# ConvFFN entry of a hybrid decoder layer: weight sums of three units and the t4 operand on GpSimd, the first unit's sums made beside the output projection

## Chip, cores and metric

The kernel runs on one core of one Trainium2 chip. The metric is the device time of one execution in microseconds, lower is better. A difference of 0.3% (5.0 us here) is about what a measurement of this kernel can tell from no change.

## What is computed

One layer of a decoder with 1024 positions of width 1024. Three token mixers run on the same normalised input, their outputs are gated and summed, one output projection adds to the residual stream, and a gated MLP with a causal convolution of width 3 (the ConvFFN) follows. The change lies where the output projection ends and the ConvFFN begins:

```
x = x + merged @ w_o[l]

h = _rmsnorm(x, g_ffn[l])
u = _causal_dwconv(h @ w_up[l], ff_conv_w[l], ff_conv_b[l])
u_val, u_gate = jnp.split(u, 2, axis=-1)
x = x + (jax.nn.silu(u_gate) * u_val) @ w_down[l]
```

All of it is float32. `w_up` is 1024 x 5632, so `h @ w_up` has 44 row blocks of 128 in the kernel's transposed layout.

## The kernel before

Activations lie transposed: 128 channels on the partitions, positions along the free dimension, in two halves of 512 positions (`hs(1)` upper, `hs(0)` lower). A float32 product is made of three matmuls (`mm3`, L142 to L144) of operands split into a rounded high part (L129, ScalarE, "ACT") and the rest (L130, VectorE, "DVE"). One matmul handles 128 x 128 weights and 512 positions.

**Output projection** (L1079 to L1111). For `h` = 1, then 0, eight row blocks `d` of `w_o` go through `proj`; `ev(d)` adds the residual (L1088), stores it and collects the sum of squares (L1094, L1095). When a half is done, `rstd_rows` makes the row scale: `rstd` sums with eight small matmuls (L158), DVE scales (L148), GpSimd ("POOL") takes the power -1/2 (L150), and `spread` writes four diagonal pieces (L170, DVE) and multiplies them with ones (L172, PE), so that the scale of each position lies on all partitions, in PSUM. For the upper half the normalised pages `full` are made beside the lower half's products (`h2_upper`, L1072); for the lower half they can be made only after its last product.

**ConvFFN** (L1118 to L1177). `ffn_up(f)` for f = 0 to 21 is a unit: it makes two row blocks (value and gate) for both halves with seven half-size products instead of eight (Strassen-Winograd, `seven`, L672 to L720). Products `au` and `bu` need only the upper half's activations. The others need four operands made of both halves, each two pages of 128 x 1024 that are then split: `t3` is the lower minus the upper half (`diff`), `t2` is `full + diff` (L1149), `t1` is L1160, `t4` is L1166; `bl` is the lower half itself (L1158). On the weight side a unit needs three sums of its 128 x 512 weight quarters and one more later, all on DVE:

```
s1 = half()
nc.vector.tensor_add(s1, a2, b2)       # L695
nc.vector.tensor_sub(a2, a1, a2)       # L696
nc.vector.tensor_sub(a1, s1, a1)       # L697
...
nc.vector.tensor_sub(b1, b1, a1)       # L708
```

(L695 is `s1`, operand of `t1`; L696 that of `t3`; L697 that of `t2`; L708 that of `bl`.) The splits of weights go through a ring of two `whi` and two `wlo` buffers (`qring`).

The first three units are written interleaved (L1142 to L1170): the upper products of all three, then t2 and t3 of units 0 and 1, then t1, then bl and t4, then the rest of unit 2. From unit 3 on the loop at L1172 runs one unit after another. The order on each engine is set by a scheduler; `tc.high_priority` moves pieces forward. All transfers are issued by the SP queue in order.

Of the kernel before, what the change touches and what calls it, by code (L numbers as in the profile page):

```python
# [11 lines left out]
F32R = mybir.dt.float32r  # L12
# [30 lines left out]
def tile_hybrid_layer(ctx: ExitStack, tc: tile.TileContext, xT, memT, vecs, w_t, w_n, w_kv, w_if,  # L43
# [20 lines left out]
    BUFS = {"h": 16, "pg": 16, "U": 5, "y": 2, "raw": 2, "whi": 2, "wlo": 2, "hf": 4, "me": 2,  # L64
# [3 lines left out]
    def T(shape, tag, dt=F32, bufs=None):  # L68
        pool = {"mw": mlp, "mst": mlp, "px": late[0]}.get(tag, sb)
        return pool.tile(shape, dt, tag=tag, name=nm(tag), bufs=bufs or BUFS[tag])  # L70

# [577 lines left out]
    RAWS = [itertools.chain(("raw", "raw", "pg"), itertools.repeat("raw"))]  # L649
# [22 lines left out]
    def seven(w1, w2, x, done, urgent=False):  # L672

        tag = next(RAWS[0])
        if tag == "me":
            a1, b1 = T([P, HALF], tag), T([P, HALF], tag)
            nc.sync.dma_start(a1, w1[:, hs(0)])
            nc.sync.dma_start(b1, w1[:, hs(1)])
        else:
            r1 = T([P, S], tag)  # L680
            nc.sync.dma_start(r1, w1)
            a1, b1 = r1[:, hs(0)], r1[:, hs(1)]
        r2 = T([P, S], "pg")
        nc.sync.dma_start(r2, w2)
        a2, b2 = r2[:, hs(0)], r2[:, hs(1)]
        L, p2 = bank(turn(2, LONG)), bank(turn(3, SHORT))
        prod(L, qring(a1), x["au"])
        c1 = wide()
        up, lo = c1[:, hs(1)], c1[:, hs(0)]
        nc.scalar.activation(up, L, AF.Copy)  # L690
        prod(p2, qring(b1), x["bu"])
        nc.vector.tensor_add(up, up, p2)
        with tc.high_priority(offset=1000 if urgent else 0):
            s1 = half()
            nc.vector.tensor_add(s1, a2, b2)  # L695
            nc.vector.tensor_sub(a2, a1, a2)  # L696
            nc.vector.tensor_sub(a1, s1, a1)  # L697
        yield
        prod(L, qring(a1, 1000 if urgent else SOON), x["t2"], False)
        c2 = wide()  # L700
        nc.scalar.activation(c2[:, hs(1)], L, AF.Copy)
        R = bank(turn(3, SHORT))
        prod(R, qring(a2, 1000 if urgent else SOON), x["t3"])
        yield
        prod(L, qring(s1), x["t1"], False)
        nc.scalar.activation(c2[:, hs(0)], L, AF.Copy)
        nc.vector.tensor_add(c2[:, hs(0)], c2[:, hs(0)], R)
        nc.vector.tensor_sub(b1, b1, a1)  # L708
        yield
        prod(L, qring(b1), x["bl"], False)  # L710
        nc.scalar.activation(lo, L, AF.Copy)
        done(0, c1)
        prod(R, qring(b2), x["t4"], False)
        nc.vector.tensor_add(c2[:, hs(1)], c2[:, hs(1)], R)  # L714
        done(1, c2)
        yield
# [360 lines left out]
    diff = [page("h") for _ in range(2)]  # L1077
    for h in (1, 0):
# [24 lines left out]
        for d in range(KT):  # L1103
            proj(w_o[d], m_hi, m_lo, ev(d), halves=(h,))
# [10 lines left out]
    RAWS[0] = itertools.chain(("raw", "raw", "me"), itertools.cycle(("px", "px", "raw", "raw", "me")))  # L1115
    LONG[:], SHORT[:] = ["pj", "tr"], ["pv", "z"]

    def ffn_up(f):  # L1118
# [15 lines left out]
        return seven(w_up[f], w_up[NF + f], fx, done, f == 0)  # L1134
# [3 lines left out]
    for n, tag in (("t2", "h"), ("t3", "pg"), ("t1", "h"), ("bl", "pg"), ("t4", "h")):  # L1138
        fd[n], fx[n] = doubles(tag)
# [273 lines left out]
```

## Time and profile before

| | |
|---|---|
| median of 3 runs | 1662.75 us (1659.86 to 1664.12) |
| profiled execution | 1658.55 us |
| its span, first to last instruction | 1656.8 us |
| granted TensorE clock, mean | 0.999 of 2.4 GHz |
| busy: PE, DVE, ACT, POOL | 1635.1, 1212.9, 823.5, 93.3 us |
| end of the last product of the output projection | 1014.25 us in the span |
| first product of unit 3 | 1074.46 us in the span |

The profiled execution is 4.2 us below the median of the runs. A PE row in the timeline starts when its matmul starts; matmuls are pipelined, so the distance of two starts is the cost of one and the busy time of one (0.39 us) is longer. On DVE too the next instruction starts some 0.07 us before the one ahead has ended, so the distance of starts is used.

### The profile page before, as it was taken

To read this page: it belongs to the slowest core of one execution; us is meant where nothing else is said; L and a number is where in the kernel's file an instruction comes from. 1 tells how busy PE (TensorE), PEld (TensorE's weight loads), DVE (VectorE), ACT (ScalarE), POOL (GpSimd) and SP (SyncE) were. 2 spreads that over 40 slices of the span, in tenths; PEclk is the share of its full clock that TensorE was granted. 3 is DMA by queue.
4 is the path that set the end of the run, shared out by engine and by line. 5 is a ranking of instruction groups with operands and counts; after the bars stand their busy time and mean duration, and the time that the engine had idled before them with its cause. 6 is when DMAs were issued, how large, how long until landed. Compare 5 with 4: busy or idle time off the path is not lost.

```text
span 1656.8 us, 21182 instructions
## 1 busy us (share of the span) xinstructions
PE 1635.1 (99%) x7911; PEld 1333.6 (80%) x7911; DVE 1212.9 (73%) x1709; ACT 823.5 (50%) x1249; POOL 93.3 (6%) x157
## 2 busy tenths in 40 slices
PE   8999999999999999999999999999999999999999
PEld 4777888887877888888788887788888888788887
DVE  5649888768764666766557558987788777889764
ACT  4547777545554454666312344555555555543431
POOL 1002222020000010100000000000000000000000
PEclk9999999999999999999999999999999999999999
DMA  8420111423333665424854453322222221586132
GB/s 297 152 65 21 39 39 53 139 84 140 130 109 124 204 182 186 135 96 135 283 189 155 137 180 122 113 103 83 71 77 79 100 77 51 181 314 241 42 125 81
DMA packets 96249, 212.68 MB, mean 128 GB/s; under 512 B 12416, under 2 KB 36224, under 8 KB 96148
## 3 DMA queue, kind: packets, MB, share of 16 engines
q1 hardware_dynamic: 96148, 211.35, 37.5%
q8 instruction: 62, 1.02, 0.2%
q14 instruction: 39, 0.32, 0.1%
HBM read 156.71 MB, written 54.61 MB: 128 GB/s over the span
## 4 chain that ended last, share of the span: by engine, by line
PE 87%; DVE 3%; ACT 1%; DMA 1%; issue 0%; POOLq 0%; POOL 0%; ACTq 0%
PE ps_pj L142 13%; PE ps_pj L143 13%; PE ps_pj L144 13%; PE ps_pv L143 6%; PE ps_pv L142 6%; PE ps_pv L144 6%; PE ps_tr L142 4%; PE ps_tr L144 4%; PE ps_tr L143 4%; PE ps_z L142 3%; PE ps_z L143 3%; PE ps_z L144 3%; PE ps_pv L443 2%; PE ps_tr L429 2%; PE ps_z L403 1%; PE ps_z L404 1%
## 5 line engine op out<-in xcount | busy, mean ns | idle before, releaser
L143 PE MATMUL ps_pj<-h,whi 128*128 128x512 f32 x620 | 242.4, 391 | 0.0
L129 ACT ACTIVATE whi<-raw 128x512 fp32r<-128x512 f32 (+1 forms) x112 | 93.7, 837 | 176.3 <-PE ps_pj L143 81.9
L142 PE MATMUL ps_pj<-h,whi 128*128 128x512 f32 x412 | 165.0, 400 | 0.0
L142 PE MATMUL ps_pj<-pg,whi 128*128 128x512 f32 x396 | 154.8, 391 | 0.3 <-DVE pg L1053 0.2
L144 PE MATMUL ps_pj<-pg,wlo 128*128 128x512 f32 x380 | 147.9, 389 | 0.0
L143 PEld LDWEIGHTS ps_pj<-h,whi 128*128 128x128 f32 x620 | 116.7, 188 | 23.0 <-DVE U L280 0.2
L144 PE MATMUL ps_pj<-h,wlo 128*128 128x512 f32 x332 | 130.3, 392 | 0.0
L812 DVE SCALAR_TENSOR_TENSOR y<-U,vec,y 128x1023 f32<-128x1023 f32 x88 | 112.3, 1278 | 8.4 <-ACT y L810 8.4
L417 DVE TENSOR_TENSOR_SCAN U<-U 128x512 f32<-128x512 f32 (+3 forms) x96 | 92.9, 1008 | 17.5 <-POOL U L412 15.8
L142 PEld LDWEIGHTS ps_pj<-h,whi 128*128 128x128 f32 x412 | 77.6, 188 | 15.5 <-issue 0.3
L130 DVE TENSOR_TENSOR wlo<-raw,whi 128x1024 fp32r<-128x1024 f32 x54 | 65.9, 1221 | 32.2 <-ACT whi L129 32.0
L142 PEld LDWEIGHTS ps_pj<-pg,whi 128*128 128x128 f32 x396 | 74.4, 188 | 16.6 <-DVE pg L1053 0.8
L144 PEld LDWEIGHTS ps_pj<-pg,wlo 128*128 128x128 f32 x380 | 71.4, 188 | 14.8 <-issue 0.2
L129 ACT ACTIVATE whi<-pg 128x512 fp32r<-128x512 f32 (+1 forms) x59 | 43.4, 738 | 72.3 <-issue 21.1
L143 PE MATMUL ps_pj<-pg,whi 128*128 128x512 f32 x188 | 73.4, 390 | 0.0
L144 PEld LDWEIGHTS ps_pj<-h,wlo 128*128 128x128 f32 x332 | 62.6, 189 | 13.2
L143 PE MATMUL ps_pv<-h,whi 128*128 128x512 f32 x164 | 64.0, 390 | 0.0
L810 ACT ACTIVATE y<-U,vec 128x1024 f32<-128x1024 f32 x44 | 54.6, 1241 | 15.8 <-DVE U L714 14.4
L144 PE MATMUL ps_pj<-h,whi 128*128 128x512 f32 x156 | 60.8, 390 | 0.0
L406 ACT ACTIVATE U<-ps_z 128x1024 f32<-128x1024 f32 (+3 forms) x48 | 39.0, 813 | 40.5 <-PE ps_z L404 32.7
L130 DVE TENSOR_TENSOR wlo<-raw,wlo 128x512 fp32r<-128x512 f32 x58 | 39.8, 686 | 22.3 <-ACT wlo L129 22.1
L144 PE MATMUL ps_tr<-pg,wlo 128*128 128x512 f32 x144 | 56.1, 389 | 0.0
(434 smaller groups left out, 4312.0 us busy)
## 6 DMA issues: line engine op xcount, KB each, us to landing
raw<-in_w_t_dram SPq DMA_DIRECT2D x29, 512.0 KB
gate_d<-U SPq DMA_DIRECT2D x24, 512.0 KB
U<-gate_d SPq DMA_DIRECT2D x24, 512.0 KB
pg<-in_w_up_dram SPq DMA_DIRECT2D x22, 512.0 KB
act_d<-y SPq DMA_DIRECT2D x22, 512.0 KB
pg<-in_w_t_dram SPq DMA_DIRECT2D x21, 512.0 KB
raw<-in_w_dn_dram SPq DMA_DIRECT2D x18, 512.0 KB
raw<-in_w_o_dram SPq DMA_DIRECT2D x16, 512.0 KB
```

The costliest lines, as they stand in the source:

```text
L129: nc.scalar.activation(hi, src, AF.Copy)
L130: (eng or nc.vector).tensor_sub(lo, src, hi.bitcast(F32))
L142: nc.tensor.matmul(out, lh, rh, start=start, stop=False, skip_group_check=more)
L143: nc.tensor.matmul(out, lh, rl, start=False, stop=False, skip_group_check=more)
L144: nc.tensor.matmul(out, ll, rh, start=False, stop=stop, skip_group_check=more)
L403: nc.tensor.matmul(z[:, a, :w], qs[a][:, ts(rb)], ks[a][:, c], start=True, stop=False)
L406: nc.scalar.activation(f[:, :, 1:w + 1], z[:, :, :w], AF.Sigmoid, scale=-0.125)
L417: nc.vector.tensor_tensor_scan(f[:, a, 1:w + 1], f[:, a, 1:w + 1], f[:, a, 1:w + 1], 1.0 if o == 0 else f[:, a, 0:1], op0=ALU.mult, op1=AL ...
L429: nc.tensor.transpose(pt[:, a, ts(j)], g[:, a, ts(j)], ident)
L443: nc.tensor.matmul(pv[64 * a:64 * a + 64, ts(rb % 4)], sbv[s // 2][:, s % 2, (2 * p + a) * 64:(2 * p + a + 1) * 64], wt[:, a, ts(j)], star ...
L810: nc.scalar.activation(out, u, AF.Identity, bias=bias, scale=taps[0])
L812: nc.vector.scalar_tensor_tensor(out[:, :S - s], u[:, s:], taps[s], out[:, :S - s], op0=ALU.mult, op1=ALU.add)
```

## The change

The three weight sums and the later difference of units 0, 1 and 2 are made by POOL instead of DVE, and so is the t4 operand (two subtractions of 128 x 1024). For unit 0 the loads of its weights, the three sums and the split of its first quarter are written into the lower half's loop of the output projection (at d = 3 and d = 6); the sums go into pages of their own (`sx`, one of the `U` pages). The pages for second weight loads alternate between the tags `h` and `pg`, and the t4 pages are one pair of each. The rest of the kernel is as before.

```diff
--- before.py
+++ after.py
@@ -61,12 +61,12 @@
         uid[0] += 1
         return f"{s}_{uid[0]}"
 
-    BUFS = {"h": 16, "pg": 16, "U": 5, "y": 2, "raw": 2, "whi": 2, "wlo": 2, "hf": 4, "me": 2,
+    BUFS = {"h": 16, "pg": 16, "U": 5, "y": 2, "sx": 1, "raw": 2, "whi": 2, "wlo": 2, "hf": 4, "me": 2,
             "mw": 4, "sm": 22, "px": 2}
     late = [None]
 
     def T(shape, tag, dt=F32, bufs=None):
-        pool = {"mw": mlp, "mst": mlp, "px": late[0]}.get(tag, sb)
+        pool = {"mw": mlp, "mst": mlp, "px": late[0], "sx": late[0]}.get(tag, sb)
         return pool.tile(shape, dt, tag=tag, name=nm(tag), bufs=bufs or BUFS[tag])
 
     def page(tag="pg", dt=F32):
@@ -646,7 +646,7 @@
 
     cyc = [0, 0, 0, 0]
     LONG, SHORT = ["pj", "tr"], ["pv", "z"]
-    RAWS = [itertools.chain(("raw", "raw", "pg"), itertools.repeat("raw"))]
+    RAWS = [itertools.chain(("raw", "raw", "pg"), itertools.repeat("raw")), itertools.repeat("pg")]
 
     def turn(i, tags):
         cyc[i] += 1
@@ -669,43 +669,50 @@
         for k in range(4):
             mm3(p, a[0][:, ts(k)], a[1][:, ts(k)], *b[k], start and k == 0, k == 3, not start)
 
-    def seven(w1, w2, x, done, urgent=False):
-
-        tag = next(RAWS[0])
+    def halves(src, tag):
+
         if tag == "me":
-            a1, b1 = T([P, HALF], tag), T([P, HALF], tag)
-            nc.sync.dma_start(a1, w1[:, hs(0)])
-            nc.sync.dma_start(b1, w1[:, hs(1)])
-        else:
-            r1 = T([P, S], tag)
-            nc.sync.dma_start(r1, w1)
-            a1, b1 = r1[:, hs(0)], r1[:, hs(1)]
-        r2 = T([P, S], "pg")
-        nc.sync.dma_start(r2, w2)
-        a2, b2 = r2[:, hs(0)], r2[:, hs(1)]
+            t = [T([P, HALF], tag) for _ in range(2)]
+            for i in range(2):
+                nc.sync.dma_start(t[i], src[:, hs(i)])
+            return t
+        r = T([P, S], tag)
+        nc.sync.dma_start(r, src)
+        return r[:, hs(0)], r[:, hs(1)]
+
+    def sums(eng, w, s1, s2):
+
+        a1, b1, a2, b2 = w
+        eng.tensor_add(s1, a2, b2)
+        eng.tensor_sub(a2, a1, a2)
+        eng.tensor_sub(s2, s1, a1)
+
+    def seven(w1, w2, x, done, eng=None, ready=None):
+
+        eng = eng or nc.vector
+        w, s1, s2, hl1 = ready or ((*halves(w1, next(RAWS[0])), *halves(w2, next(RAWS[1]))), None, None, None)
+        a1, b1, a2, b2 = w
         L, p2 = bank(turn(2, LONG)), bank(turn(3, SHORT))
-        prod(L, qring(a1), x["au"])
+        prod(L, hl1 or qring(a1), x["au"])
         c1 = wide()
         up, lo = c1[:, hs(1)], c1[:, hs(0)]
         nc.scalar.activation(up, L, AF.Copy)
         prod(p2, qring(b1), x["bu"])
         nc.vector.tensor_add(up, up, p2)
-        with tc.high_priority(offset=1000 if urgent else 0):
-            s1 = half()
-            nc.vector.tensor_add(s1, a2, b2)
-            nc.vector.tensor_sub(a2, a1, a2)
-            nc.vector.tensor_sub(a1, s1, a1)
+        if not ready:
+            s1, s2 = half(), a1
+            sums(eng, w, s1, s2)
         yield
-        prod(L, qring(a1, 1000 if urgent else SOON), x["t2"], False)
+        prod(L, qring(s2, 1000 if ready else SOON), x["t2"], False)
         c2 = wide()
         nc.scalar.activation(c2[:, hs(1)], L, AF.Copy)
         R = bank(turn(3, SHORT))
-        prod(R, qring(a2, 1000 if urgent else SOON), x["t3"])
+        prod(R, qring(a2, 1000 if ready else SOON), x["t3"])
         yield
         prod(L, qring(s1), x["t1"], False)
         nc.scalar.activation(c2[:, hs(0)], L, AF.Copy)
         nc.vector.tensor_add(c2[:, hs(0)], c2[:, hs(0)], R)
-        nc.vector.tensor_sub(b1, b1, a1)
+        eng.tensor_sub(b1, b1, s2)
         yield
         prod(L, qring(b1), x["bl"], False)
         nc.scalar.activation(lo, L, AF.Copy)
@@ -745,9 +752,9 @@
     def halves_of(k0, h):
         return [(hh[k][:, hs(h)], hl[k][:, hs(h)]) for k in range(k0, k0 + 4)]
 
-    def doubles(tag):
-
-        d = [[T([P, S], tag, F32R) for _ in range(2)] for _ in range(2)]
+    def doubles(*tags):
+
+        d = [[T([P, S], tag, F32R) for _ in range(2)] for tag in (tags[0], tags[-1])]
         return d, [(d[k // 2][0][:, hs(k % 2)], d[k // 2][1][:, hs(k % 2)]) for k in range(4)]
 
     gx = {"au": halves_of(0, 1), "bu": halves_of(4, 1), "bl": halves_of(4, 0), "t3": halves_of(0, 0)}
@@ -1075,6 +1082,7 @@
 
     bau, bbu = quarter("pg"), quarter("h")
     diff = [page("h") for _ in range(2)]
+    early = None
     for h in (1, 0):
         x1s = []
         acc = half()
@@ -1101,6 +1109,14 @@
             return f
 
         for d in range(KT):
+            if h == 0 and d == 3:
+
+                w = (*halves(w_up[0], "me"), *halves(w_up[NF], "h"))
+                early = w, T([P, HALF], "sx"), wide()[:, :HALF]
+                sums(nc.gpsimd, *early)
+            if h == 0 and d == 6:
+                early += (pair("U"),)
+                split(w[0], *early[3])
             proj(w_o[d], m_hi, m_lo, ev(d), halves=(h,))
             if h == 0 and d > 0:
                 if d == 1:
@@ -1112,7 +1128,7 @@
 
 
     act_d = dtile([NF // 2, 2, P, S], "act_d")
-    RAWS[0] = itertools.chain(("raw", "raw", "me"), itertools.cycle(("px", "px", "raw", "raw", "me")))
+    RAWS[:] = itertools.cycle(("raw", "raw", "px", "px", "me")), itertools.cycle(("h", "pg", "pg", "h"))
     LONG[:], SHORT[:] = ["pj", "tr"], ["pv", "z"]
 
     def ffn_up(f):
@@ -1131,12 +1147,12 @@
                     nc.sync.dma_start(act_d[f // 2, :, :, hs(f % 2)].rearrange("h p r -> p h r"),
                                       ys[0].rearrange("p (h r) -> p h r", h=2))
 
-        return seven(w_up[f], w_up[NF + f], fx, done, f == 0)
+        return seven(w_up[f], w_up[NF + f], fx, done, nc.gpsimd if f < 3 else None, early if f == 0 else None)
 
 
     fd, fx = {}, {"au": bau, "bu": bbu}
-    for n, tag in (("t2", "h"), ("t3", "pg"), ("t1", "h"), ("bl", "pg"), ("t4", "h")):
-        fd[n], fx[n] = doubles(tag)
+    for n, tags in (("t2", ("h",)), ("t3", ("pg",)), ("t1", ("h",)), ("bl", ("pg",)), ("t4", ("h", "pg"))):
+        fd[n], fx[n] = doubles(*tags)
     units = [ffn_up(f) for f in range(NF)]
     rows = rstd_rows(kept[0], HALF)
     first = units[:3]
@@ -1163,7 +1179,7 @@
         next(u)
     for j in range(2):
         split(x1p[2 + j], *fd["bl"][j])
-        nc.vector.tensor_sub(full[2 + j], full[2 + j], full[j])
+        nc.gpsimd.tensor_sub(full[2 + j], full[2 + j], full[j])
         split(full[2 + j], *fd["t4"][j])
     next(first[0])
     middle(first[2])
```

### The order of instructions

POOL, from the last rows of the mixers to the end, before; `sm` is a row scale (L150):

```order
L150 TENSOR_TENSOR sm_6178<-sm_6176,nhalf 128x8
L150 TENSOR_TENSOR sm_6495<-sm_6493,nhalf 128x8
L150 TENSOR_TENSOR sm_6805<-sm_6803,nhalf 128x8
L150 TENSOR_TENSOR sm_8388<-sm_8386,nhalf 128x4
L150 TENSOR_TENSOR sm_8678<-sm_8676,nhalf 128x4
```

and now, from the row scale of the upper half (`sm_8388`) on; `sm_8692` is that of the lower half, L686 to L688 and L715 are the weight sums, L1182 is t4 (the three sums of unit 0 stand in front of this piece):

```order
L150 TENSOR_TENSOR sm_8388<-sm_8386,nhalf 128x4
L715 TENSOR_TENSOR me_8442<-me_8442,U_8448 128x512
L150 TENSOR_TENSOR sm_8692<-sm_8690,nhalf 128x4
L686 TENSOR_TENSOR hf_8772<-h_8735 128x512
L686 TENSOR_TENSOR hf_8815<-pg_8778 128x512
L687 TENSOR_TENSOR h_8735<-raw_8733,h_8735 128x512
L687 TENSOR_TENSOR pg_8778<-raw_8776,pg_8778 128x512
L688 TENSOR_TENSOR raw_8733<-hf_8772,raw_8733 128x512
L688 TENSOR_TENSOR raw_8776<-hf_8815,raw_8776 128x512
L715 TENSOR_TENSOR raw_8733<-raw_8733 128x512
L715 TENSOR_TENSOR raw_8776<-raw_8776 128x512
L1182 TENSOR_TENSOR pg_7990<-pg_7990,pg_7988 128x1024
```

Fourteen instructions came onto POOL: four for unit 0, of which three stand ahead of the upper half's row scale, and ten in a block behind the lower half's (the second L1182 follows the last row shown).

DVE, from the row scale of the lower half to the operands, before (`ps_tr_8685` is the spread row scale, `h_8000` and `h_8001` are `diff`, `pg_7988` is the first page of `full`):

```order
L695 TENSOR_TENSOR hf_8726<-pg_8689 128x512
L170 TENSOR_SCALAR hf_8680<-ident,sm_8678 128x128
L696 TENSOR_TENSOR pg_8689<-raw_8687,pg_8689 128x512
L170 TENSOR_SCALAR hf_8680<-ident,sm_8678 128x128
L697 TENSOR_TENSOR raw_8687<-hf_8726,raw_8687 128x512
L170 TENSOR_SCALAR hf_8680<-ident,sm_8678 128x128
L130 TENSOR_TENSOR wlo_8781<-me_8773,wlo_8781 128x512
L695 TENSOR_TENSOR hf_8769<-pg_8732 128x512
L695 TENSOR_TENSOR hf_8814<-pg_8777 128x512
L1148 TENSOR_TENSOR h_8000<-h_8000,ps_tr_8685 128x512 x2
L1148 TENSOR_TENSOR h_8001<-h_8001,ps_tr_8685 128x512
L1149 TENSOR_TENSOR pg_7988<-pg_7988,h_8000 128x1024
```

and now (`ps_tr_8699` is the row scale; `pg_8670` and `pg_8672` are low parts of t3, `h_8666` and `h_8668` those of t2):

```order
L170 TENSOR_SCALAR hf_8694<-ident,sm_8692 128x128 x4
L1164 TENSOR_TENSOR h_8000<-h_8000,ps_tr_8699 128x512 x2
L1164 TENSOR_TENSOR h_8001<-h_8001,ps_tr_8699 128x512
L1165 TENSOR_TENSOR pg_7988<-pg_7988,h_8000 128x1024
L1164 TENSOR_TENSOR h_8001<-h_8001,ps_tr_8699 128x512
L130 TENSOR_TENSOR pg_8670<-h_8000,pg_8669 128x1024
L130 TENSOR_TENSOR whi_8833<-U_8448,whi_8833 128x512
L130 TENSOR_TENSOR h_8666<-pg_7988,h_8665 128x1024
L1165 TENSOR_TENSOR pg_7989<-pg_7989,h_8001 128x1024
L130 TENSOR_TENSOR wlo_8851<-h_8445,wlo_8851 128x512
L130 TENSOR_TENSOR pg_8672<-h_8001,pg_8671 128x1024
L130 TENSOR_TENSOR h_8668<-pg_7989,h_8667 128x1024
```

The sums between and behind the L170 rows are gone, and from the row scale to the second low part of t2 (`h_8668`) there are only the operands and two weight splits.

PE, around the matmul that reads the second page of t2, before (`h_8654` is the low part of that page; from its first row to the first product of unit 3 there are 149 matmuls):

```order
L142 MATMUL ps_pv_8849<-pg_8657,whi_8850 128x512
L143 MATMUL ps_pv_8849<-pg_8658,whi_8850 128x512
L144 MATMUL ps_pv_8849<-pg_8657,whi_8850 128x512
L143 MATMUL ps_tr_8691<-h_8654,wlo_8832 128x512
L144 MATMUL ps_tr_8691<-h_8653,wlo_8832 128x512
L142 MATMUL ps_tr_8691<-h_8653,wlo_8832 128x512
L143 MATMUL ps_tr_8691<-h_8654,wlo_8832 128x512
```

and now (`h_8668`; from its first row to the first product of unit 3 there are 158 matmuls):

```order
L144 MATMUL ps_tr_8701<-h_8665,whi_8833 128x512
L142 MATMUL ps_tr_8701<-h_8667,whi_8833 128x512
L142 MATMUL ps_pv_8850<-pg_8669,wlo_8851 128x512
L143 MATMUL ps_pv_8850<-pg_8670,wlo_8851 128x512
L144 MATMUL ps_pv_8850<-pg_8669,wlo_8851 128x512
L143 MATMUL ps_tr_8701<-h_8668,whi_8833 128x512
L144 MATMUL ps_tr_8701<-h_8667,whi_8833 128x512
L142 MATMUL ps_tr_8701<-h_8667,whi_8833 128x512
L143 MATMUL ps_tr_8701<-h_8668,whi_8833 128x512
```

That matmul stands nine places further forward.

## Rows read from the trace of the kernel before

**Rows 1.** The page, part 1: busy time of PE, share, instructions.

```profile
PE 1635.1 (99%) x7911; PEld 1333.6 (80%) x7911; DVE 1212.9 (73%) x1709; ACT 823.5 (50%) x1249; POOL 93.3 (6%) x157
```

**Rows 2.** Busy time by stretches: length, PE, PEld, DVE, ACT, POOL, PEclk, DMA share, GB/s.

```profile
980.00:1000.00 20.00, 20.00 (x91) 16.32 (x91) 17.72 (x28) 10.97 (x16) 1.89 (x1) 1.00 0.57 189
...
1020.00:1030.00 10.00, 9.54 (x41) 7.25 (x40) 10.00 (x18) 5.05 (x8) 0.00 (x0) 1.00 0.00 0
1030.00:1040.00 10.00, 8.89 (x36) 6.10 (x35) 10.00 (x14) 3.37 (x6) 0.00 (x0) 1.00 0.00 0
1040.00:1050.00 10.00, 7.94 (x34) 5.95 (x33) 9.78 (x14) 5.51 (x8) 0.00 (x0) 1.00 0.01 2
```

**Rows 3.** Timeline of PE: start, us, engine, line, instruction [idle before, releaser].

```profile
1022.61 1.12 PE L172 MATMUL ps_tr<-hf,ones 128*128 128x512 f32 x2 [0.46 <-DVE hf L170]
...
1035.41 0.50 PE L143 MATMUL ps_tr<-h,wlo 128*128 128x512 f32 x1
...
1044.60 0.50 PE L142 MATMUL ps_tr<-pg,wlo 128*128 128x512 f32 x1 [0.88 <-DVE px L1158]
...
1048.79 0.50 PE L142 MATMUL ps_tr<-h,wlo 128*128 128x512 f32 x1 [1.18 <-ACT U L701]
...
1074.46 0.39 PE L142 MATMUL ps_pj<-pg,whi 128*128 128x512 f32 x1
...
1075.14 0.39 PE L142 MATMUL ps_pj<-pg,whi 128*128 128x512 f32 x1
```

**Rows 4.** Timeline of DVE, from the row scale to the t4 operand.

```profile
1018.21 0.16 DVE L148 TENSOR_SCALAR sm<-ps_tr 128x4 f32<-128x4 f32 x1 [0.60 <-PE ps_tr L158]
...
1019.87 0.29 DVE L170 TENSOR_SCALAR hf<-ident,sm 128x128 f32<-128x128 f32 x1 [0.90 <-POOL sm L150]
...
1024.28 1.87 DVE L1148 TENSOR_TENSOR h<-h,ps_tr 128x512 f32<-128x512 f32 x3
1026.07 1.21 DVE L1149 TENSOR_TENSOR pg<-pg,h 128x1024 f32<-128x1024 f32 x1
...
1034.15 1.21 DVE L130 TENSOR_TENSOR h<-pg,h 128x1024 fp32r<-128x1024 f32 x1
1035.28 0.67 DVE L692 TENSOR_TENSOR U<-U,ps_pv 128x512 f32<-128x512 f32 x1
...
1052.33 2.35 DVE L1166 TENSOR_TENSOR pg<-pg,pg 128x1024 f32<-128x1024 f32 x2
```

**Rows 5.** Timeline of POOL, the row scale of the lower half.

```profile
1018.52 1.32 POOL L150 TENSOR_TENSOR sm<-sm,nhalf 128x4 f32<-128x4 f32 x1 [35.53 <-DVE sm L148]
```

**Rows 6.** POOL's instructions on three lines: shortest/median/longest in ns, starts, forms.

```profile
L412 POOL TENSOR_SCALAR_AFFINE_SELECT U<-U x64: 400/407/2706, 120.1 to 305.4; 128x256 f32<-128x256 f32 x64
...
L857 POOL TENSOR_SCALAR_AFFINE_SELECT me<-me x8: 634/640/1689, 368.6 to 637.4; 128x512 f32<-128x512 f32 x8
...
L565 POOL TENSOR_TENSOR mw<-mw,mw x1: 452/452/452, 363.3 to 363.3; 32x128 f32<-32x128 f32 x1
```

**Rows 7.** Timeline of POOL and DVE where instructions of both overlap, two places.

```profile
277.18 0.95 POOL L412 TENSOR_SCALAR_AFFINE_SELECT U<-U 128x256 f32<-128x256 f32 x1 [0.51 <-ACT U L407]
...
276.70 1.23 DVE L417 TENSOR_TENSOR_SCAN U<-U 128x512 f32<-128x512 f32 x1 [1.27 <-POOL U L412]
...
277.85 1.36 DVE L417 TENSOR_TENSOR_SCAN U<-U 128x512 f32<-128x512 f32 x1
...
441.10 1.69 POOL L857 TENSOR_SCALAR_AFFINE_SELECT me<-me 128x512 f32<-128x512 f32 x1 [70.76 <-ACT y L810]
...
441.01 1.28 DVE L812 SCALAR_TENSOR_TENSOR y<-U,cw,y 128x1023 f32<-128x1023 f32 x1 [0.44 <-ACT y L810]
```

**Rows 8.** Timeline of the SP queue in the output projection.

```profile
927.92 0.33 SPq L135 DMA_DIRECT2D raw<-in_w_o_dram  x1
...
931.77 0.33 SPq L1089 DMA_DIRECT2D x_d<-U  x1
...
996.53 0.33 SPq L135 DMA_DIRECT2D raw<-in_w_o_dram  x1
```

## The prediction

> **What bounds the kernel now.** The page comes first: PE is busy for 99% of the span [rows 1], so a change off PE can only win back the places where PE waits. The table by stretches shows where they are [rows 2]: from 1020 to 1050 us PE is busy 9.54, 8.89 and 7.94 of each 10 us, and in the same stretches DVE has no pause (10.00, 10.00, 9.78). The granted clock is 1.00 throughout, so 2.4 GHz, and no term below comes from it. That is the entry of the ConvFFN: the last product of the output projection is done, DVE has to make the operands of both halves, the weight sums and the splits at once, and PE runs out of operands.
>
> PE's timeline gives the size. A matmul costs 0.227 us (three from 1074.46 to 1075.14 [rows 3]). From 1035.41, where PE reads the second page of t2, to the first product of unit 3 at 1074.46 there are 149 matmuls, 33.8 us of work in 39.05: 5.3 us of waiting, with 0.88 us for L1158 and 1.18 us for an eviction among it [rows 3]. Before 1035.41 there is 0.46 us for the row scale and some tenths more. About 6 us is all that can be won; 5.0 us (0.3%) is what a measurement can tell. From unit 3 on PE has no wait, so the start of unit 3 is the mark: what moves it moves the end.
>
> **The change, part by part.** *Off DVE.* Twelve instructions of 128 x 512 (L695 to L697 and L708 of three units) at 0.60 us each (L1148 takes 1.79 from its start to the next row for three [rows 4]) are 7.2 us, and the two L1166 2.3 us [rows 4]: 9.5 us of DVE.
>
> *Moved ahead.* Unit 0's three sums run on POOL beside the output projection, where POOL has nothing else to do. The split of its first quarter, 0.60 us on DVE, moves from the end of the lower half's loop into its middle; DVE has 2.3 of 20 us free there [rows 2], which covers it, and without that cover it costs 0.6. The weight load goes into the SP queue ahead of the load of block 3 of `w_o` (927.92 [rows 8]), and waits until PE frees an `h` page at the end of the branch products, one product (24 matmuls, 5.4 us) before the store at 931.77 [rows 8], so about 926: nothing behind it is late, and block 3's weights are wanted only two products after that store. A prefetch for unit 5 stands ahead of the load of block 7 (996.53 [rows 8]); it waits for unit 0's early split, which in DVE's order stands some products ahead of block 7. All of this I cost at nothing. Unit 0's last difference (L715) falls just before the row scale and can hold DVE up for 1 us; that shift lies inside the gaps allowed for below.
>
> *Onto POOL.* Behind the row scale, POOL issues eight sums of 128 x 512 and two subtractions of 128 x 1024 without a pause. No row shows a two-input POOL instruction of that size. The one-input rows go 407 ns for 256 and 634 for 512 elements [rows 6], so about 0.17 us fixed and 0.9 ns per element; the only plain two-input row is 452 ns for 128 elements [rows 6], 0.28 above the fixed part, 2.2 ns per element. From below a sum costs 0.64 us (the one-input row), from above I have no row and take 1.6 (the two-input row ran on 32 partitions and may be mild). I take the two-input row: 0.17 + 1.13 = 1.30 us per sum, 2.43 per subtraction.
>
> *What POOL does to DVE.* Alone, 15 us of POOL against 9.5 us of DVE would be harmless, but the two are not independent. At 277.18 a POOL instruction that needs 0.41 us takes 0.95: it starts inside a DVE scan (276.70 to 277.93) and ends 0.20 us after it. The next scan, queued right behind, takes 1.36 instead of 1.23 [rows 7]. At 441.10 a 0.64 us POOL instruction takes 1.69 and ends 0.49 us after a DVE instruction with two SBUF operands [rows 7]. So each waits for the other to finish reading, in turn, when DVE reads two operands from SBUF. L1148 and the U sums read one operand from PSUM; the rows show no such wait against those.
>
> The Trainium skill states the same contention more strictly ("SBUF — State Buffer", Who interferes with whom): the second read port is a lock that is held for the whole instruction. The scan at 277.85 speaks for less, 0.13 us late behind an instruction of 0.41 [rows 7]. By the page each POOL instruction would hold DVE for its 1.30 and 2.43 us, 15.3 in all; by the row only for the part that streams, 1.13 and 2.26 us, 13.6 in all. I go by the row and keep the other as a rival.
>
> *The sum.* The row scale leaves POOL at 1019.84 [rows 5]. From there to the second page of t2 DVE has 8.0 us of work with two SBUF operands (two L1165 and four splits of 1.14 us, two splits of 0.60), and POOL's ten instructions, 13.6 us, alternate with them: four fall in the time of L170, the spread and L1164, and one goes ahead of each of the next six. Both through the port: 1019.84 + 8.0 + 13.6 = 1041.4, plus some 0.6 us for gaps at the start (four L170 and POOL's fixed parts): 1042.0. Before, that page was complete at 1035.28 [rows 4] and PE used it at 1035.41 [rows 3]. Now PE uses it at 1042.1, stands nine matmuls earlier in its order, and has 158 to go: 35.8 us, unit 3 at 1077.9.
>
> Does anything wait after that? POOL is done at about 1040, so DVE is free of it: the second page of t1 is 13.7 us of DVE work later (eleven instructions of 512 at 0.60 to 0.66, six of 1024 at 1.14: 1055.7) and wanted 62 matmuls later (1056.2); the last t4 split another 5.3 us later (1061.0) and wanted at about 1063. Both just make it. The mark moves from 1074.46 to 1077.9: **3.4 us slower, which is inside the 0.3%**. The change trades scattered waits of 6 us for one wait of 9 at t2. The profiled execution, 1658.55, would become 1662; it lies 4.2 under the median of the runs, so against the median 1662.75 I forecast **1666 us**. With 1.2 to 1.4 us for a sum, and 0 to 1.2 us for the gaps, this case spans 1664.3 to 1667.9.
>
> **The rivals.** *POOL holds longer* (slower). The place is the same, the ten instructions behind the row scale. If a sum holds the port for all of its 1.30 us, the 13.6 us become 15.3, the mark moves by 5.1 us: 1667.9. (The Trainium skill's page on SBUF, named above, states this form.) If a sum takes 1.6 us (1.43 of it streaming, 2.86 for t4), 17.2 us, 7.0 slower: 1669.8. It decides from 15.2 us of holding, 1.43 us per sum. For it: the only two-input row has 32 partitions. Against it: POOL's one-input rows are the same on 128.
>
> *POOL is milder* (inside the noise, somewhat faster). At the lower bound, 0.64 us per sum, the ten hold 0.47 and 0.94 us, 5.6 in all. Then t2 is complete at about 1035.1 (its own 10.4 us of DVE work after the row scale at about 1022.3, and some 2.4 of holding), the mark at 1071.0, 3.5 us faster: 1659.2.
>
> *The port is not disputed here* (faster). If DVE's back-to-back instructions keep POOL out, or the reads interleave, DVE runs as its order says: the four L170 follow each other without the sums (0.8 us, done at 1020.7), the spread ends 1.9 us earlier, t2 is complete at 1032.7, PE hardly waits, and the mark comes at about 1069: 5.5 faster, 1657.2. For it: a POOL instruction once waited 2.7 us [rows 6], longer than one DVE instruction of 1.2 us lasts. Against it: the median of 407 ns comes from places without dispute, and at 277.85 POOL got in between two queued scans.
>
> *The change moves nothing of note*: POOL starts so late that PE waits for sums instead of operands. The order excludes most of it: POOL's block stands right behind the row scale (1019.84), some 16 us before PE wants a sum of unit 1 or 2. It would give 1662.75 within a microsecond.
>
> **How the numbers follow.** The port in turn, as worked out (1664.3 to 1667.7): 0.55. Longer holding, over 5.0 us slower: 0.16. Milder, within 5 us either way: 0.18. Undisputed or nearly, over 5.0 us faster: 0.11. So faster 0.11, same 0.73, slower 0.16. The range leaves out most of the undisputed case and the far end of the longer one: 1658 to 1669.5.
>
> **What would show it.** Right: L686 to L688 and L1182 of the changed kernel at 1.2 to 1.4 and 2.3 to 2.5 us or more, each longer one ending just after a DVE instruction; DVE splits beside them at 1.7 to 2.3 us instead of 0.68 and 1.21; the second t2 split done at 1041 to 1043; one PE wait of 6 to 8 us there, few after it; unit 3 at 1077 to 1079. Wrong: splits of 1.21 us beside running sums, or t2 complete before 1036, and with it a mark before 1074. If the mark moves as forecast and the end does not, a later stage has given time back, which nothing here foresees.

## The result and the profile after

The changed kernel takes **1664.45 us** (median of 22 runs, 1662.67 to 1668.32), the kernel before 1660.95 on the same chip (22 runs, 1659.11 to 1664.82): a ratio of 1.0020, interval 1.0014 to 1.0026, so 3.5 us more and inside the 0.3%. The profiled execution is 1666.73 us, its span 1665.0.

The page's busy line, which answers to [rows 1]:

```profile
PE 1637.7 (98%) x7911; PEld 1335.8 (80%) x7911; DVE 1215.5 (73%) x1695; ACT 824.2 (50%) x1249; POOL 113.3 (7%) x171
```

DVE has 14 instructions fewer and is 2.6 us busier: an instruction that has started and is held up counts as busy (the rows of DVE below). The table by stretches, which answers to [rows 2] (columns: PE, PEld, DVE, ACT, POOL with counts, PE clock, DMA share, GB/s):

```profile
1020.00:1030.00 10.00, 5.48 (x25) 3.82 (x23) 6.95 (x9) 0.63 (x1) 7.92 (x7) 0.84 0.03 12
1030.00:1040.00 10.00, 10.00 (x37) 7.77 (x36) 9.37 (x9) 5.11 (x7) 5.73 (x4) 0.82 0.00 0
1040.00:1050.00 10.00, 7.22 (x26) 5.26 (x25) 10.00 (x11) 2.21 (x3) 2.77 (x1) 0.86 0.00 0
1050.00:1060.00 10.00, 10.00 (x44) 8.10 (x43) 7.96 (x9) 6.20 (x9) 0.00 (x0) 0.97 0.01 2
```

Two things are new. PE is busy for 5.48 us of the first stretch, with 25 matmuls, and DVE, at 6.95 us, is not full there either: PE and DVE wait in turn. And the granted clock is 0.82 to 0.86 in the first three stretches, which means that part of each ran at 1.2 GHz instead of 2.4. The mean clock of each of the 22 runs is 0.996 to 0.998 (the profiled one 0.997), so this comes back in every one. In the second stretch PE looks full, but 37 matmuls are 8.4 us of work at 0.227.

PE's timeline of the same execution shows the two waits, slow matmuls behind each, and the mark (first product of unit 3):

```profile
1028.52 2.07 PE L172 MATMUL ps_tr<-hf,ones 128*128 128x512 f32 x2 [4.52 <-DVE hf L170]
1030.82 0.63 PE L143 MATMUL ps_tr<-pg,U 128*128 128x512 f32 x1
1031.24 0.63 PE L144 MATMUL ps_tr<-pg,U 128*128 128x512 f32 x1
1045.97 0.50 PE L143 MATMUL ps_tr<-h,whi 128*128 128x512 f32 x1 [2.78 <-DVE h L130]
1047.28 0.63 PE L142 MATMUL ps_pv<-pg,wlo 128*128 128x512 f32 x1
1047.71 0.63 PE L143 MATMUL ps_pv<-pg,wlo 128*128 128x512 f32 x1
1083.86 0.39 PE L142 MATMUL ps_pj<-pg,wlo 128*128 128x512 f32 x1
```

The same executions are compared by a stretch that I call the **entry**: from unit 0's first matmul, right behind the output projection (1014.25 before, 1017.88 here), to the mark. It is 60.21 us before [rows 3] and 65.98 here, 5.8 more. The 3.6 us between the two starts had come up bit by bit (0.9 us at the 200th matmul, near 66 us; 2.0 at the 3500th, near 660). Over all ten profiles of this study the start lies between 1014.25 and 1017.88, with no order by kernel: run e5, the kernel before up to here, has 1016.26, and run e1, in which only units 1 and 2 and t4 differ from the changed kernel, 1014.36. So I take it for the spread of executions.

The cause of both waits stands in POOL's timeline, whose first row answers to [rows 5] (the number in brackets is the idle time before, and what ended it):

```profile
1022.08 1.40 POOL L150 TENSOR_TENSOR sm<-sm,nhalf 128x4 f32<-128x4 f32 x1 [3.31 <-DVE sm L148]
1023.44 1.28 POOL L686 TENSOR_TENSOR hf<-h 128x512 f32<-128x512 f32 x1
1024.67 1.27 POOL L686 TENSOR_TENSOR hf<-pg 128x512 f32<-128x512 f32 x1
...
1034.48 2.42 POOL L1182 TENSOR_TENSOR pg<-pg,pg 128x1024 f32<-128x1024 f32 x1 [1.16 <-DVE pg L1165]
1040.92 2.77 POOL L1182 TENSOR_TENSOR pg<-pg,pg 128x1024 f32<-128x1024 f32 x1 [4.03 <-DVE pg L1165]
```

and DVE's, which answers to [rows 4] (L1164 is the L1148 of before):

```profile
1023.51 4.95 DVE L170 TENSOR_SCALAR hf<-ident,sm 128x128 f32<-128x128 f32 x4 [0.91 <-POOL sm L150]
1030.63 1.88 DVE L1164 TENSOR_TENSOR h<-h,ps_tr 128x512 f32<-128x512 f32 x3 [2.17 <-PE ps_tr L172]
1034.92 3.05 DVE L130 TENSOR_TENSOR pg<-h,pg 128x1024 fp32r<-128x1024 f32 x1
1041.37 3.41 DVE L130 TENSOR_TENSOR pg<-h,pg 128x1024 fp32r<-128x1024 f32 x1
1044.70 1.21 DVE L130 TENSOR_TENSOR h<-pg,h 128x1024 fp32r<-128x1024 f32 x1
```

Behind the row scale (L150) POOL starts its first sum at 1023.44, DVE its first diagonal piece (L170) at 1023.51. From there each of the four pieces stands behind one sum: 4.95 us for the four, and PE, which needs the scale, waits 4.52. DVE in turn waits 2.17 us for PE's spread (L172), whose two matmuls run at the low clock. Then two splits of 1.21 us take 3.05 and 3.41, because they stand behind the two t4 subtractions; the second page of t2 is complete at 1045.84, and PE waits 2.78 for it. L1164, which reads PSUM and one SBUF operand, takes its usual 1.88 for three although POOL runs beside it.

### The profile page after: what moved, and what is told of

Its sections match the earlier page's. It is cut to its first block, busy times and chain, and to the rows that moved or that the text cites. A ratio compares the mean times of both kernels' runs of the same rounds, so it can differ in the third digit from the quotient of the medians.

```text
span 1665.0 us, 21200 instructions
## 1 busy us (share of the span) xinstructions
PE 1637.7 (98%) x7911; PEld 1335.8 (80%) x7911; DVE 1215.5 (73%) x1695; ACT 824.2 (50%) x1249; POOL 113.3 (7%) x171
## 4 chain that ended last, share of the span: by engine, by line
PE 86%; DVE 3%; DMA 1%; ACT 1%; issue 1%; POOL 0%; SPq 0%; POOLq 0%; ACTq 0%
PE ps_pj L142 13%; PE ps_pj L143 13%; PE ps_pj L144 13%; PE ps_pv L142 6%; PE ps_pv L143 6%; PE ps_pv L144 6%; PE ps_tr L143 4%; PE ps_tr L144 4%; PE ps_tr L142 4%; PE ps_z L142 3%; PE ps_z L143 3%; PE ps_z L144 3%; PE ps_pv L443 2%; PE ps_tr L429 2%; PE ps_z L403 1%; PE ps_z L404 1%
## 5 line engine op out<-in xcount | busy, mean ns | idle before, releaser
L143 PE MATMUL ps_pj<-h,whi 128*128 128x512 f32 x540 | 211.1, 391 | 0.0
L144 PE MATMUL ps_pj<-h,wlo 128*128 128x512 f32 x412 | 160.9, 391 | 0.0
L142 PE MATMUL ps_pj<-h,whi 128*128 128x512 f32 x332 | 133.7, 403 | 0.7 <-DVE U L1062 0.7
L143 PEld LDWEIGHTS ps_pj<-h,whi 128*128 128x128 f32 x540 | 101.6, 188 | 19.9 <-issue 0.2
L417 DVE TENSOR_TENSOR_SCAN U<-U 128x512 f32<-128x512 f32 (+3 forms) x96 | 92.7, 1006 | 17.0 <-POOL U L412 15.3
L144 PEld LDWEIGHTS ps_pj<-h,wlo 128*128 128x128 f32 x412 | 77.4, 188 | 16.4
L142 PEld LDWEIGHTS ps_pj<-h,whi 128*128 128x128 f32 x332 | 62.4, 188 | 13.1 <-DVE U L1062 1.1
L143 PE MATMUL ps_tr<-h,whi 128*128 128x512 f32 x176 | 68.7, 391 | 2.8 <-DVE h L130 2.8
L129 ACT ACTIVATE whi<-pg 128x512 fp32r<-128x512 f32 (+1 forms) x46 | 35.3, 770 | 62.5 <-PE ps_pv L143 18.2
L142 PE MATMUL ps_pj<-h,wlo 128*128 128x512 f32 x156 | 61.5, 394 | 0.0
L143 PE MATMUL ps_pj<-h,wlo 128*128 128x512 f32 x156 | 60.8, 390 | 0.0
L144 PE MATMUL ps_pv<-pg,wlo 128*128 128x512 f32 x150 | 58.9, 392 | 0.0
```

The costliest lines, as they stand in the source:

```text
L129: nc.scalar.activation(hi, src, AF.Copy)
L142: nc.tensor.matmul(out, lh, rh, start=start, stop=False, skip_group_check=more)
L143: nc.tensor.matmul(out, lh, rl, start=False, stop=False, skip_group_check=more)
L144: nc.tensor.matmul(out, ll, rh, start=False, stop=stop, skip_group_check=more)
L417: nc.vector.tensor_tensor_scan(f[:, a, 1:w + 1], f[:, a, 1:w + 1], f[:, a, 1:w + 1], 1.0 if o == 0 else f[:, a, 0:1], op0=ALU.mult, op1=AL ...
```

## The experiments

Two theories. *Port*: POOL's reads and DVE's instructions take turns, and the ten POOL instructions behind the row scale make the whole loss. *Row scale*: only the four caught L170 cost something, by the wait and the clock behind it. Ratios are to the kernel before on the same chip. "Entry" is the stretch defined above, from one profile of each kernel; line numbers are those of the changed kernel (e6 has five lines more from L705 on and eight more from L718 on, so its rows show L1164 as L1172; e5 is the kernel before with one line more).

| run | sums on POOL behind the row scale | t4 | entry, us | ratio (interval) |
|---|---|---|---|---|
| before | none | DVE | 60.21 | 1 |
| after | 8 | POOL | 65.98 | 1.0020 (1.0014 to 1.0026) |
| e1 | none (unit 0's on POOL) | DVE | 57.65 | 0.9977 (0.9967 to 0.9987) |
| e2 | none (all on DVE) | DVE | 57.67 | 0.9976 (0.9967 to 0.9985) |
| e3 | 8 | DVE | 62.02 | 1.0001 (0.9992 to 1.0010) |
| e4 | 8, and L170 on POOL | POOL | 68.92 | 1.0041 (1.0028 to 1.0054) |
| e5 | none (before, ring turned) | DVE | 60.25 | 0.9991 (0.9982 to 1.0000) |
| e6 | 8 copies | DVE | 56.92 | 0.9983 (0.9974 to 0.9993) |
| e7 | none | POOL | 61.85 | 0.9994 (0.9983 to 1.0004) |
| e8 | 4 | DVE | 60.60 | 0.9992 (0.9983 to 1.0001) |

**e1 and e2: the early unit alone.** Both keep unit 0's early loads, sums and split; e1 makes its sums on POOL, e2 on DVE, and units 1, 2 and t4 are on DVE as before. The edit of e1:

```diff
-        return seven(w_up[f], w_up[NF + f], fx, done, nc.gpsimd if f < 3 else None, early if f == 0 else None)
+        return seven(w_up[f], w_up[NF + f], fx, done, nc.gpsimd if f < 1 else None, early if f == 0 else None)
...
-        nc.gpsimd.tensor_sub(full[2 + j], full[2 + j], full[j])
+        nc.vector.tensor_sub(full[2 + j], full[2 + j], full[j])
```

e2 has the same for t4, and for all sums:

```diff
-                sums(nc.gpsimd, *early)
+                sums(nc.vector, *early)
...
-        return seven(w_up[f], w_up[NF + f], fx, done, nc.gpsimd if f < 3 else None, early if f == 0 else None)
+        return seven(w_up[f], w_up[NF + f], fx, done, None, early if f == 0 else None)
```

> The entry is counted from the first matmul of unit 0 to the first of unit 3: 60.2 us before, 66.0 us after. Port theory (POOL's reads and DVE's two-operand instructions take turns, and the ten POOL instructions behind the row scale cost the entry): with only unit 0's four sums on POOL, beside the projection, the entry loses 2.4 us of DVE work against before and has no dispute: entry 57 to 59 us, time 1 to 3 us below before. Row-scale theory (only the four diagonal pieces caught behind sums cost anything): the same, 57 to 59. Rival (the new loads, pages or the early work itself cost the time, not POOL): entry stays at 65 to 66, time 3 to 4 us above before.

> The change with every sum and t4 on DVE; only unit 0's weights are still loaded and summed beside the projection. Port theory: POOL's early sums cost nothing, so this equals the run with unit 0 alone on POOL within 0.5 us, entry 57 to 59. If POOL's early sums hold DVE up just ahead of the row scale (the last one, L715), this one is 0.5 to 1 us shorter. Rival (loads and pages): entry 65 to 66.

Both entries are 2.5 us shorter than before, near the 2.4 us of DVE work that left this stretch, and both kernels are faster than before and after (0.23 and 0.24% below before, less than the 0.3% that a measurement is said to tell, but with intervals clear of 1). Four instructions of unit 0 on POOL, while DVE has room, cost nothing (57.65 against 57.67); their place ahead of the row scale is what wins. DVE's timeline of e2 shows the pieces without POOL beside them:

```profile
1022.87 0.88 DVE L170 TENSOR_SCALAR hf<-ident,sm 128x128 f32<-128x128 f32 x4 [0.90 <-POOL sm L150]
```

**e3: the eight sums without t4.**

```diff
-        nc.gpsimd.tensor_sub(full[2 + j], full[2 + j], full[j])
+        nc.vector.tensor_sub(full[2 + j], full[2 + j], full[j])
```

> The change with t4 back on DVE: eight POOL sums remain behind the row scale. Port theory: 4.5 us of holding fewer before the second page of t2, which is complete about 4 us earlier than in the changed kernel; the diagonal pieces still take about 5 us. Entry 61 to 63, time 3 to 4 us below the changed kernel, about that of before. Row-scale theory: entry 65 to 66 still, time as the changed kernel within 1 us.

Entry 62.02, 4.35 over e2, and L170 as in the changed kernel (4.95 for four). PE's wait, from its timeline of e3:

```profile
1028.25 2.07 PE L172 MATMUL ps_tr<-hf,ones 128*128 128x512 f32 x2 [4.55 <-DVE hf L170]
```

So of the changed kernel's 65.98, the eight sums cost 4.35 and t4 the other 3.96. Matmul by matmul against e2, the 4.35 are 4.04 of a later row scale and 2.45 of matmuls at the low clock behind it, less 2.1 because the later waits of e2 shrink.

**e7: t4 without the sums.** As e2, with only this line of the changed kernel left:

```diff
-        nc.vector.tensor_sub(full[2 + j], full[2 + j], full[j])
+        nc.gpsimd.tensor_sub(full[2 + j], full[2 + j], full[j])
```

> As e2 (all weight sums on DVE, unit 0 early), but the two subtractions of the fourth operand on POOL, as in the changed kernel. Port theory: the row scale and its four L170 run free (L172 wait 0.4 us), the clock stays full there, but the two subtractions take 2.3 us each of DVE's splits behind L1165, so the second page of t2 is 3 to 4.5 us later than in e2 and PE waits there: entry 60 to 62 us against 57.7, that is 1660 to 1662. Rival (the fourth operand cost 4 us in the changed kernel only because the eight sums had used up the slack): entry below 58.7, no more than 1 us over e2.

Entry 61.85, inside the port theory's range; 4.18 over e2, so the two costs add up (57.67 + 4.35 + 4.18 = 66.2, measured 65.98). DVE's timeline of e7 shows where DVE loses: each subtraction catches a split that takes 0.69 elsewhere.

```profile
1028.79 2.60 DVE L130 TENSOR_TENSOR whi<-U,whi 128x512 fp32r<-128x512 f32 x1
1031.33 1.21 DVE L1165 TENSOR_TENSOR pg<-pg,h 128x1024 f32<-128x1024 f32 x1
1032.46 1.21 DVE L130 TENSOR_TENSOR h<-pg,h 128x1024 fp32r<-128x1024 f32 x1
1033.59 2.87 DVE L130 TENSOR_TENSOR wlo<-h,wlo 128x512 fp32r<-128x512 f32 x1
```

That is 1.9 and 2.2 us, 4.1 together. That this is nearly the 4.18 is chance: in e2 the second page of t2 was ready 1.3 us before PE came to it, so PE reads it only 2.77 us later than there,

```profile
1037.65 0.50 PE L143 MATMUL ps_tr<-h,whi 128*128 128x512 f32 x1 [2.27 <-DVE h L130]
```

and matmuls at the low clock behind this wait add 1.5 (0.3 is won back later). This run also falls against the row-scale theory: L170 runs free (PE waits 0.44 there), and the loss begins at t2.

**e4: L170 out of the way.** The lower half's four pieces are made by POOL, ahead of its sums.

```diff
-            nc.vector.tensor_scalar(dg[:, ts(t)], ident, r[:, t:t + 1], None, op0=ALU.mult)
+            (eng or nc.vector).tensor_scalar(dg[:, ts(t)], ident, r[:, t:t + 1], None, op0=ALU.mult)
...
-    rows = rstd_rows(kept[0], HALF)
+    rows = rstd_rows(kept[0], HALF, nc.gpsimd)
```

> The change with the four diagonal pieces of the lower half's row scale made by POOL, which stands ahead of its sums and so can't be caught by them. Row-scale theory: the 4.5 us wait of PE for the spread row scale shrinks to under 1.5 us, the clock stays at full level there, entry about 59 to 60, time 5 us below the changed kernel. Port theory: the spread comes earlier too, but the ten POOL instructions still alternate with DVE ahead of t2, which is complete only 0 to 2 us earlier; PE's wait moves from the row scale to t2, entry 63 to 65.

The row scale reaches PE 2.5 us earlier relative to the entry's start, and the entry is 2.9 us *longer* (68.92). The row-scale theory falls; the port theory had the place right (t2) and the number too low. DVE's timeline of e4, and PE's wait at t2, tell why:

```profile
1035.59 2.31 DVE L130 TENSOR_TENSOR h<-pg,h 128x1024 fp32r<-128x1024 f32 x1
1037.83 2.31 DVE L1165 TENSOR_TENSOR pg<-pg,h 128x1024 f32<-128x1024 f32 x1
1040.07 2.83 DVE L130 TENSOR_TENSOR wlo<-h,wlo 128x512 fp32r<-128x512 f32 x1
1042.82 3.35 DVE L130 TENSOR_TENSOR pg<-h,pg 128x1024 fp32r<-128x1024 f32 x1
1046.10 1.21 DVE L130 TENSOR_TENSOR h<-pg,h 128x1024 fp32r<-128x1024 f32 x1
...
1047.37 0.79 PE L143 MATMUL ps_tr<-h,whi 128*128 128x512 f32 x1 [5.59 <-DVE h L130]
```

The sums that the four pieces had covered now stand in the way of the splits instead. The prediction's own sum, without the 0.6 us for L170 and with 2.35 for POOL's four pieces, gives it: row scale 1023.23 + 8.0 of DVE + 13.6 of POOL + 2.35 = 1047.2, and the page is complete at 1047.24. Counted from the entry's start, PE reads it 1.65 us later than in the changed kernel. The rest of the 2.9 us lies behind: three matmuls more stand behind it here (0.7 us), and more matmuls run at the low clock (0.6). A split of 1.14 us followed 2.24 later (1035.59 to 1037.83) puts one sum's turn at 1.10 us; alone a sum takes 1.27, or 1.22 from start to start.

**e6: a shorter read.** As e3, but units 1 and 2 get copies with one input in place of sums, so their weight sums are left out.

```diff
-            sums(eng, w, s1, s2)
+            if eng is nc.gpsimd:
+                eng.tensor_copy(s1, a2)
+                eng.tensor_copy(a2, a1)
+                eng.tensor_copy(s2, s1)
+            else:
+                sums(eng, w, s1, s2)
...
-        eng.tensor_sub(b1, b1, s2)
+        if eng is nc.gpsimd and not ready:
+            eng.tensor_copy(b1, s2)
+        else:
+            eng.tensor_sub(b1, b1, s2)
```

> As e3 (fourth operand on DVE), but POOL's eight instructions of units 1 and 2 are copies with one input instead of sums and differences: the weight sums of these two units are left out. POOL's one-input rows took 0.63 us for 512 elements. Port theory (POOL's reading and DVE's two-operand instructions take turns, for the time that POOL streams): each of the four L170 is caught behind a copy of half a sum's length, about 0.65 us apiece instead of 1.29, PE waits about 2.4 us less at L172 (2.1 instead of 4.5), and the entry takes 59 to 60 us instead of 62.0. If one-input reads do not contend at all: L170 as in e1 (0.8 us for four), entry 57.7. If any POOL instruction holds DVE up alike, whatever it reads: L170 at 1.29 and entry 62.

POOL's and DVE's first rows, and PE's wait:

```profile
1022.49 0.61 POOL L705 COPY hf<-h 128x512 f32<-128x512 f32 x1
1023.04 0.61 POOL L705 COPY hf<-pg 128x512 f32<-128x512 f32 x1
```

```profile
1022.57 2.28 DVE L170 TENSOR_SCALAR hf<-ident,sm 128x128 f32<-128x128 f32 x4 [0.91 <-POOL sm L150]
...
1024.90 1.12 PE L172 MATMUL ps_tr<-hf,ones 128*128 128x512 f32 x2 [1.88 <-DVE hf L170]
```

A copy of 0.61 us holds each piece by half as much (0.55 from start to start, 1.22 behind a sum): the pieces follow the length of POOL's read, as the port theory says, and PE waits 1.88 (expected 2.1). But the entry, 56.92, is below the expected 59 to 60 and even below e2. Against e3, from which I had worked it out, I had left out the clock: the row scale comes 2.66 us earlier (expected 2.4), and the clock stays at 2.4 GHz behind the wait, which gives the other 2.45 of the 5.10. It is below e2 because DVE is rid of the eight instructions: POOL is done at 1026.99, before L1165 (1027.86), and the two waits of 1.2 us that e2 still has (behind L1174 and L708) shrink to one of 0.56. The run's ratio is less good than its entry; one profile against the median of ten runs, I leave that open.

**e8: half the sums.** As e3, with only unit 1 on POOL.

```diff
-        return seven(w_up[f], w_up[NF + f], fx, done, nc.gpsimd if f < 3 else None, early if f == 0 else None)
+        return seven(w_up[f], w_up[NF + f], fx, done, nc.gpsimd if f < 2 else None, early if f == 0 else None)
```

> As e3, but only units 0 and 1 on POOL, so four POOL instructions behind the row scale instead of eight. If the place decides (each of the four L170 is caught behind one POOL instruction, whatever follows): the four pieces still take about 5 us, L172 still waits 4.5 us, and the entry is 61 to 62 us, as in e3. If the count decides (each sum costs its share): half of e3's loss, entry about 59.8.

60.60, between the two: over e2 the row scale comes 2.0 us later and matmuls at the low clock add 1.5, less 0.6 later on. Neither place nor count alone decides: unit 1's sums depend on each other, so POOL starts the next one some 0.08 us after the one before has ended, and a piece of DVE's slips in. One at a time, L170 takes 1.29, 0.27, 1.28 and 0.27:

```profile
1021.44 2.89 DVE L170 TENSOR_SCALAR hf<-ident,sm 128x128 f32<-128x128 f32 x4 [0.91 <-POOL sm L150]
1024.24 1.77 DVE L686 TENSOR_TENSOR hf<-pg 128x512 f32<-128x512 f32 x1
1026.05 1.65 DVE L687 TENSOR_TENSOR pg<-raw,pg 128x512 f32<-128x512 f32 x1
```

In the changed kernel the sums of two units alternate, POOL starts the next one without that pause (1.22 us from start to start), and takes every second turn.

**e5: the down projection.** After unit 3 the kernel before loses 1.35 us that the changed kernel doesn't: from the mark to the 1800th matmul behind it, 409.49 us before, 408.15 after. ScalarE's timeline at the first weight split of the down projection, before and after (`whi` of 128 x 1024):

```profile
1436.42 1.06 ACT L129 ACTIVATE whi<-raw 128x1024 fp32r<-128x1024 f32 x1 [0.77 <-PE ps_pj L144]
```

```profile
1443.10 1.06 ACT L129 ACTIVATE whi<-raw 128x1024 fp32r<-128x1024 f32 x1 [1.60 <-PE ps_pv L144]
```

and PE's wait before, for that split:

```profile
1437.53 0.50 PE L142 MATMUL ps_tr<-pg,whi 128*128 128x512 f32 x1 [1.15 <-ACT whi L129]
```

Before, the `whi` page came free with the last product of unit 21 (`ps_pj`), after, with the one ahead of it (`ps_pv`). The ring hands out `whi` and `wlo` in turn; unit 0's early split has a page of its own (`U`), so the splits behind it are one step over, and the last one takes `wlo`. To test it, the kernel before got one step and nothing else:

```diff
+    cyc[0] += 1
     units = [ffn_up(f) for f in range(NF)]
```

> The kernel before, with the ring that hands out whi and wlo pages to the weight splits of the ConvFFN turned on by one step. In the kernel before, the last weight split ahead of the down projection took a whi page, PE read it until 1436, and the down projection's first split, which also wants whi, came late: PE waited 1.15 us at 1437.53. In the changed kernel unit 0's first split has a page of its own, the ring is one step behind, the last split took wlo, and that wait is gone. Ring theory: the step alone removes this wait, the entry stays at 60.2 us, and the time is 1.1 us below the kernel before (about 0.07%). Rival (the wait went with the other pages of the weights): it stays, and the time is the same.

The wait of 1.15 us is gone, the entry is the same (60.25), and the split is released by `ps_pv`:

```profile
1435.75 1.06 ACT L129 ACTIVATE whi<-raw 128x1024 fp32r<-128x1024 f32 x1 [1.60 <-PE ps_pv L144]
```

The stretch behind the mark is 408.13, and 408.14 or 408.15 in all runs with the early split, so their times have the 1.35 us too. The ratio of e5, 0.9991 (0.9982 to 1.0000), agrees with 0.07%, though it can hardly be told from 1. The profile settles the cause, the times only don't contradict it.

## Why the prediction was right

The forecast was 3.4 us slower, within the 0.3%, for the port in turn. It came out at 3.5, but that it came so near is luck: terms that I didn't have, of opposite sign, are in it. (1666 stood on a median before of three runs, 1662.75; on that of 22 runs, 1660.95, the same 3.4 gives 1664.4. The upper end of the case is 1667.9 in one place and 1667.7 in another; nothing hangs on it.)

*Right.* **The price of POOL:** 1.30 per sum and 2.43 per subtraction; measured 1.27 to 1.29, and 2.42 for the subtraction that did not wait (2.77 for the other). The two-input row of 128 elements [rows 6] was the right one to take. **The mechanism:** POOL's instructions and DVE's take turns when DVE reads two operands from SBUF (e7, e4), and the place is the stretch from the row scale to t2. **The early unit and the loads** hold nothing up (e1, e2), and behind t2 no PE wait of 0.2 us or more follows. **The rivals:** held for its whole length, the 13.6 us would be 15.3; the turn of 1.10 in e4, against 1.22 to 1.27 for a sum, speaks against that. The Trainium skill ("SBUF — State Buffer", Who interferes with whom) states that form: a lock for the whole instruction. The undisputed port is excluded by every row of L170.

*Right by luck: the time of the second page of t2.* It was forecast for 1042.0, with the 3.6 us by which this entry starts later 1045.6; it was complete at 1045.84. But its two halves were wrong by nearly the same amount. From the row scale to the first L1165 the sum has four turns of POOL and 0.6 us, 5.1 in all; it took 8.95 (1023.48 to 1032.43): four held L170, DVE's wait of 2.17 for the spread, and three L1164 behind it. From there it has six turns and 8.0 us of DVE, 17.0; it took 13.4, because POOL ran on through that wait and L1164, and only its last sum and the two subtractions were left. Nor did POOL's block run without a pause: each subtraction waited for its L1165 (1.16 and 4.03 us). So DVE did not pay for all ten instructions, as the forecast had it. In e4 the halves fit better: 6.4 us against 6.9, and 17.6 against 17.0.

*Wrong: "four L170 and POOL's fixed parts, 0.6 us".* I counted only DVE instructions with two SBUF operands as taking part. L170 has one operand in SBUF and a column of scalars, and is caught all the same, 1.29 us instead of 0.28. The Trainium skill's section just named lists `tensor_scalar` among the instructions that can take the shared pair; the trace agrees, and I had not applied it. So PE's one wait at t2 (6 to 8 us among the forecast's signs, 9 in its sum) became two, 4.52 at the row scale and 2.78 at t2.

*Wrong: "no term comes from the clock".* Behind each wait the granted clock fell to 1.2 GHz. Behind the first, the matmuls came 0.43 us apart instead of 0.227 until 1033.4. The wait at t2 then covered that, but for the slow spread: L1164 starts 2.11 us behind L172 here and 1.16 in e6, at the full clock. Behind the second, nothing covered them: from 1045.97 to the mark there are 158 matmuls, as forecast, in 37.9 us instead of 35.8. These 2.1 us, 1.6 of them from matmuls 0.43 us apart, and 0.2 at t2 are the difference between 3.4 and 5.8.

*Not priced: the early unit's own gain.* I put 6 us down as all that could be won and let the port take it; that moving unit 0's work ahead wins 2.5 us by itself I did not work out. It is in the 65.98, under 8.3 us of loss to POOL.

*Not foreseen: the ring.* The 1.35 us given back at the down projection (e5). 5.8 less 1.35 is 4.4, against a measured 3.5 (3.3 us by the ratio's middle). The same sum, entry against that of before less 1.35, gives the ratios of the other runs within 1.3 us, but for e6 (1.8). What is left stays open: each entry comes from one profile, each ratio from many runs.

## What to carry to other kernels

In this kernel, instructions on GpSimd were free beside VectorE only while VectorE had room or waited itself. Where VectorE is the bound, each GpSimd read that one of its SBUF instructions meets costs it about the time that the read streams, and a short instruction on the chain to PE pays as much as a long one. Move work ahead of the bound stage, on whichever engine (e1 and e2, 0.23 and 0.24% faster), rather than to another engine within it. And follow a delay on VectorE through to PE: it costs less where PE has the operand in hand, and more where PE's wait is followed by a lower clock (e7). When one allocation leaves a ring, look at who shares the ring's last step with the stage that follows.

## What the runs showed of the hardware

**A 128 x 128 `tensor_scalar` can cost 1.29 us.** Alone it takes 0.28, 0.20 from start to start (e2); behind a GpSimd sum it ends 0.08 us after the sum (after). Behind a copy of 0.61 us it takes 0.61 to 0.64 (e6). What it costs depends on how closely GpSimd's instructions follow each other: in e8, with 0.08 us between them, every second piece got through in 0.27.

**In these runs the granted clock fell with waits of a few microseconds, and that is a term of its own.** PE's idle time before L172 or t2, and the granted clock of the stretch that holds the matmuls behind it: 4.52 us, 0.82 (after, 1030 to 1040); 4.55, 0.82 (e3); 2.78, 0.86 (after, 1040 to 1050); 2.48, 0.83 (e8); 2.27, 0.89 (e7); 1.88, 1.00 (e6); waits of 1.2 us, 1.00 (e2). The rows of e8, e7 and e6, with PE's wait in e8, are the following:

```profile
1024.38 1.13 PE L172 MATMUL ps_tr<-hf,ones 128*128 128x512 f32 x2 [2.48 <-DVE hf L170]
...
1020.00:1030.00 10.00, 7.52 (x25) 5.38 (x24) 9.06 (x11) 1.07 (x2) 6.91 (x5) 0.83 0.00 0
```

```profile
1040.00:1050.00 10.00, 8.84 (x35) 6.90 (x33) 9.23 (x15) 3.97 (x6) 0.00 (x0) 0.89 0.00 1
```

```profile
1020.00:1030.00 10.00, 8.12 (x38) 6.17 (x37) 7.27 (x13) 2.75 (x5) 5.85 (x9) 1.00 0.00 0
```

So a wait of this length costs more than itself: 1.5 us more in e7 and e8, 2.45 in e3. The scattered waits of the kernel before (six of 0.2 to 1.2 us, 3.6 in all) left the clock at 1.00 [rows 2].
